# A transposition through TensorE: fewer semaphore instructions and copies on VectorE, and a semaphore by which TensorE tells that a chunk is copied

## The chip, the core and the metric

The kernel runs on one core of one Trainium2 chip. The metric is the device time of one execution in microseconds (us), lower is better. "Span" is the time from the first to the last instruction of a profiled execution; the device time lies a little above it.

## The reference

```python
def setup_inputs():
    return {"x": np.random.randn(8192, 8192).astype(np.float32)}

def reference(x):
    return np.transpose(x)
```

268 MB are read and 268 MB are written; every element moves to its mirrored place.

## The kernel before, in words

**Tiling.** The input is read in 128 chunks (`T`), t = 0 to 127. A chunk is 128 rows by 4096 columns, 2 MB. In SBUF it is 16 pieces (`NR`) of 256 columns. TensorE transposes a piece with two 128x128 matmuls against the identity (every second column each), so a chunk is 32 transposes. Pieces 0 to 7 land in one half of PSUM (`pss[0]`), pieces 8 to 15 in the other (`pss[1]`). ScalarE copies the first half out, VectorE the second (`copies`, L265).

**Why the copies go to two places.** A store should write long rows. Store w therefore collects one piece from each of 16 successive chunks. The piece of chunk t that completes store t is the direct cell: it goes straight from PSUM into the store's place in `arena`. It lies in ScalarE's half if t mod 16 is below 8, else in VectorE's. All other pieces wait in `slots`. When a store's last chunk is near, VectorE copies its 15 waiting pieces from `slots` to `arena` (`gather`, L240), some 2.4 us in two or three copies. A gather first waits until the stores that held its place have landed (`free`, on `s_st`).

**One queue.** SyncE issues all transfers in the order of the list `order`: store t-1, then load t+2, and at the end 15 shorter stores that flush what is left (`flush`). A load takes one of three places in `arena`, free once TensorE has transposed the chunk that stood there. The store of chunk t waits for its direct cell (`s_x`).

**TensorE's order in chunks 12 to 125** (`transposes`, L350; `E` = 12, `LAST` = 126): it waits until ScalarE has released its half of PSUM (`s_free[0]`), then VectorE its half (`s_free[1]`, L358); it runs two idle matmuls of 512 columns (L360), takes ScalarE's go (`s_go`, L362) and the load (`s_ld`, L363), and transposes (L366). After 4, 8, 12 and 16 pieces it raises `s_pe`: these are the four steps that the copies wait for.

**ScalarE's fillers.** From chunk 24 on (`CALM`), ScalarE waits for the load of chunk u, writes the identity twice over its own half of PSUM (L401, 2048 columns each), and only then gives `s_go`. In program order on ScalarE the fillers of chunk u stand behind its copies of chunk u-1.

**Semaphores around the copies.** Each engine counts its finished copies in `s_cp`, one per chunk, waits for its own count, and then releases its half of PSUM with an instruction of its own:

```python
                cp.then_inc(s_cp[e], 1)
                if t < T - 1:
                    eng.wait_ge(s_cp[e], t + 1)
                    eng.sem_inc(s_free[e], 1)
```

A gather waits for both counts ahead of its first copy. A chunk's copies wait for the gather's count (`s_g`) ahead of everything else.

Of the kernel before, what the change touches and what calls it, by code (L numbers as in the profile page):

```python
# [40 lines left out]
def kernel(  # L41
# [5 lines left out]
    nc = tc.nc  # L47
# [6 lines left out]
    NR = 16  # L54
# [3 lines left out]
    T = (M // J) * CH  # L58
    PIECE = B * P
    FIN = 38  # L60
    E = 12
# [13 lines left out]
    def lane(w):  # L75
        return w % W if w < T else W + w - T
# [14 lines left out]
    order = []  # L91
# [19 lines left out]
    for k in order:  # L111
        if k[0] == "L":
            wanted.append((due[k] - 2 * NR, k, NR, due[k] + 2 * NR))
        elif k[1] < T:
            w = k[1]
# [6 lines left out]
    for _, k, size, until in sorted(wanted):  # L122
        if k[0] == "L":
            o = spot(k[1])
        else:
            w = k[1]
            lo = NIN * NR if w < T - 2 else 0
            hi = END
            late = lambda o: max([f for _, a, z, f in users if a < o + size and o < z], default=0)
# [7 lines left out]
            o = min(at, key=lambda o: (late(o), o))  # L137
# [10 lines left out]
    with tc.tile_critical():  # L148
# [8 lines left out]
        s_st = [nc.alloc_semaphore(f"s_st{k}") for k in range(2 * W - 1)]  # L157
        s_pe = nc.alloc_semaphore("s_pe")
# [2 lines left out]
        s_g = nc.alloc_semaphore("s_g")  # L161
        s_go = nc.alloc_semaphore("s_go")
        s_rest = nc.alloc_semaphore("s_rest")
        s_x = [nc.alloc_semaphore("s_xa"), nc.alloc_semaphore("s_xv")]

        stored = [0] * (2 * W - 1)
# [3 lines left out]
        gathered = [0]  # L170
        closed = {}
        shut = [0, 0]

# [61 lines left out]
        def direct(w, t):  # L237
            return t == w or (t == T - 1 and w == T)

        def gather(w, upto):  # L240
            from_ = begun.get(w, max(0, w - W + 1))
            begun[w] = upto
            for u in before.pop(("S", w), []):
                free(nc.vector, u)
            r = w % NR
            runs = runs_of(
                [(slot(r, t), *place(w, t)) for t in range(from_, upto)],
                lambda a, b: (b[0] - a[0], P) if b[1] - a[1] == P and a[2] == b[2] else None,
            )
            if runs:  # L250
                for k in range(2):
                    nc.vector.wait_ge(s_cp[k], upto)  # L252
            for v in runs:
                so, do, dist = v[0]
                gap = v[1][0] - so if len(v) > 1 else PIECE
                cp = nc.vector.tensor_copy(  # L256
                    out=ap(arena, do, [[P, len(v)], [dist, B], [1, P]]),
                    in_=ap(slots, so, [[gap, len(v)], [P, B], [1, P]]),
                )
            if runs:  # L260
                cp.then_inc(s_g, 1)
                gathered[0] += 1
            ready[w] = gathered[0]

        def copies(t):  # L265
            for e, eng in enumerate((nc.scalar, nc.vector)):
                need = max(ready[w] for w in (t, T) if w in ready and direct(w, t))
                if need:
                    eng.wait_ge(s_g, need)
                first, last = e * NR // 2, (e + 1) * NR // 2  # L270
                cells_ = []
                for g in range(first, last):
                    r = range_at(t, g)
                    w = t + (r - t) % NR
                    n = next(n for n, hi in enumerate(steps(t)) if g < hi)
                    cells_.append((g, w, None if direct(w, t) else slot(r, t), n))
                runs = runs_of(
                    cells_, lambda a, b: None if None in a + b or a[3] != b[3] else b[2] - a[2]
                )
                runs.sort(key=lambda v: v[0][1] != t)  # L280
                for v in runs:
                    g, w, o, n = v[0]
                    eng.wait_ge(s_pe, 4 * t + n + 1)  # L283
                    u = g - first
                    i = pss[e][:, u * PIECE:(u + len(v)) * PIECE]
                    if o is None:
                        off, dist = place(w, t)
                        dst = ap(arena, off, [[dist, B], [1, P]])
                        i = i.rearrange("p (b i) -> p b i", b=B)
                    else:  # L290
                        gap = v[1][2] - o if len(v) > 1 else PIECE
                        dst = ap(slots, o, [[gap, len(v)], [1, PIECE]])
                        i = i.rearrange("p (l i) -> p l i", l=len(v))
                    cp = eng.copy(out=dst, in_=i) if e == 0 else eng.tensor_copy(out=dst, in_=i)  # L294
                    if w == t:
                        cp.then_inc(s_x[e], 1)
                        shut[e] += 1
                        closed[t] = (s_x[e], shut[e])
                cp.then_inc(s_cp[e], 1)
                if t < T - 1:  # L300
                    eng.wait_ge(s_cp[e], t + 1)
                    eng.sem_inc(s_free[e], 1)  # L302

        def store(w):
            if w < T:
                nc.sync.wait_ge(*closed[w])
            else:
                if w == T:
                    nc.sync.wait_ge(s_cp[0], T)
                nc.sync.wait_ge(s_g, ready[w])  # L310
            pieces = []
            base = home["S", w] * PIECE
            r = w % NR
            for a, z in parts(w):
                s, c = divmod(a, CH)
                rows = (z - a) * P
                j0 = s * J + r * PIECE
                dst = out[j0:j0 + PIECE, c * P:c * P + rows]
                dst = dst.rearrange("(q b) i -> q b i", q=P)
                pieces.append((rows, dst, arena[:, base:base + B * rows]))  # L320
                base += B * rows
            for rows, dst, src in sorted(pieces, key=lambda v: -v[0]):
                if w:
                    st = wide_dma(nc, nc.sync, "qSPDynamicHW", dst, src)
                else:
                    st = nc.sync.dma_start(out=dst, in_=src.rearrange("q (b i) -> q b i", b=B))
                st.then_inc(s_st[lane(w)], 16)
                stored[lane(w)] += 16
            done[w] = stored[lane(w)]
# [20 lines left out]
        def transposes(t):  # L350
            o = home["L", t]
            for g in range(NR):
                h, u = divmod(g, NR // 2)
                if u == 0 and not (h and E <= t < LAST):
                    nc.tensor.sem_inc(s_free[h], -1).wait_op(s_free[h], 1, "sem-ge")
                if g == 0:
                    if E <= t < LAST:
                        nc.tensor.sem_inc(s_free[1], -1).wait_op(s_free[1], 1, "sem-ge")  # L358
                        for _ in range(IDLE):
                            nc.tensor.matmul(out=pss[1][:, :4 * P], lhsT=ident, rhs=four, start=True, stop=True)  # L360
                    if E <= t < LAST:
                        nc.tensor.sem_inc(s_go, -1).wait_op(s_go, 1, "sem-ge")  # L362
                    nc.tensor.sem_inc(s_ld[o], -16).wait_op(s_ld[o], 16, "sem-ge")  # L363
                q = (o + range_at(t, g)) * PIECE
                for b in range(B):
                    tr = nc.tensor.transpose(  # L366
                        pss[h][:, (u * B + b) * P:(u * B + b + 1) * P],
                        arena[:, q + b:q + PIECE - B + b + 1:B],
                        ident,
                    )  # L370
                if g + 1 in steps(t):
                    tr.then_inc(s_pe, 1)
# [19 lines left out]
        def work(t):  # L392
            while worked[0] <= t:
                u = worked[0]
                if E <= u < LAST:
                    if u < CALM:
                        nc.scalar.sem_inc(s_go, 1)
                    else:
                        nc.scalar.wait_ge(s_ld[home["L", u]], 16)
                    for k in range(REST if u >= CALM else 0):  # L400
                        cp = nc.scalar.copy(  # L401
                            out=pss[0].rearrange("p (k i) -> p k i", i=P), in_=ap(ident, 0, [[0, J // 2 // P], [1, P]])
                        )
                        if k < REST - 1:
                            cp.then_inc(s_rest, 1)
                            rested[0] += 1
                            nc.scalar.wait_ge(s_rest, rested[0])
                    if u >= CALM:
                        cp.then_inc(s_go, 1)
                gather(u, u)  # L410
                if u == T - 1:
                    gather(T, u)
                copies(u)
                worked[0] += 1
# [10 lines left out]
                    gather(k[1], T)  # L425
                store(k[1])
        for k in range(2 * W - 1):
            nc.sync.wait_ge(s_st[k], stored[k])


# [28 lines left out]
```

## Time and profile before

| | |
|---|---|
| device time, three runs | 1265.3, 1285.86, 1289.19 us; median 1285.86 |
| profiled execution | 1273.26 us, span 1271.5 us |
| TensorE, matmuls / weight loads | 861.4 us (68%) / 655.3 us (52%) |
| VectorE | 615.1 us (48%), 715 instructions |
| ScalarE | 638.9 us (50%), 606 instructions |
| DMA | 537.07 MB, 422 GB/s over the span |
| mean granted TensorE clock | 0.869 |

How to read it: busy shares are means over the whole span. Names in rows are those of the program: L256 is the gather's copy, L294 the copies out of PSUM, L401 the fillers, L360 the idle matmuls, L366 the transposes, L28 a store's issue, L203 a load's. In a row of the timeline stand the start, the busy time, engine, line, operation and count, and in brackets the idle time ahead of it and what ended it. In a row of stretches stand, after the stretch and its length, busy times and instruction counts of PE, weight loads, VectorE, ScalarE and GpSimd, then the granted TensorE clock, the DMA share and GB/s.

### The profile page before, as it was taken

The numbers are of one execution on the slowest core, as the hardware profiler recorded it, in microseconds if no ns is written. First come the engines' busy times: TensorE is split into PE (matmuls) and PEld (weight loads), VectorE is DVE, ScalarE is ACT, GpSimd is POOL, SyncE is SP. The second block draws the span as 40 slices with busy tenths as digits, with TensorE's granted clock in tenths as the row PEclk, the third lists the DMA queues.
The fourth block names the chain that finished last, engine by engine and source line by source line (L and its number), as shares of the span: only waits on it lengthen the run. The fifth ranks groups of instructions, "written<-read, shape, count | busy, mean of one in ns | idle before, by whom it ended". The sixth has DMA issues, their size and how long they took to land. (4 is left out here: it accounts for less than half of the span.)

```text
span 1271.5 us, 12053 instructions
## 1 busy us (share of the span) xinstructions
PE 861.4 (68%) x4552; PEld 655.3 (52%) x4552; DVE 615.1 (48%) x715; ACT 638.9 (50%) x606; POOL 0.7 (0%) x6
## 2 busy tenths in 40 slices
PE   6766767777667766777767777667767667767630
PEld 5755645555545555555555555545555555455420
DVE  3554554455444454444545444554445545445481
ACT  2321224556565566555655565565655656555510
POOL 0000000000000000000000000000000000000000
PEclk9898887889898889888898888988898988889875
DMA  9999999999999999999999999999999999999998
GB/s 387 425 425 426 426 428 426 431 431 430 432 429 431 433 430 430 430 432 421 416 428 428 431 430 431 430 431 432 415 429 430 421 409 404 423 430 432 405 400 335
DMA packets 41332, 537.07 MB, mean 422 GB/s; under 512 B 4576, under 2 KB 5216, under 8 KB 8288
## 3 DMA queue, kind: packets, MB, share of 16 engines
q1 hardware_dynamic: 41312, 536.89, 99.8%
q14 instruction: 18, 0.15, 0.0%
q8 instruction: 2, 0.03, 0.0%
HBM read 268.44 MB, written 268.44 MB: 422 GB/s over the span
## 5 line engine op out<-in xcount | busy, mean ns | idle before, releaser
L366 PEld LDWEIGHTS ps<-ident,arena 128*128 128x128 f32 x4096 | 565.0, 212 | 238.2 <-issue 238.1
L366 PE MATMUL ps<-ident,arena 128*128 128x128 f32 x4096 | 579.9, 306 | 119.9 <-PEq L363 119.1
L256 DVE COPY arena<-slots 128x2048 f32<-128x2048 f32 (+7 forms) x316 | 304.3, 1012 | 483.3 <-DMA out_dram<-arena 473.7
L360 PE MATMUL ps<-ident 128*128 128x512 f32 x456 | 287.5, 764 | 242.2 <-PEq L358 242.2
L401 ACT COPY ps<-ident 128x2048 f32<-128x2048 f32 x204 | 381.4, 1869 | 52.8 <-DMA arena<-in_x_dram 49.0
L294 ACT COPY slots<-ps 128x1024 f32<-128x1024 f32 (+2 forms) x335 | 238.6, 781 | 252.2 <-DVE arena L256 220.8
L294 DVE COPY slots<-ps 128x512 f32<-128x512 f32 (+2 forms) x336 | 289.3, 913 | 64.7 <-PE ps L366 63.5
L360 PEld LDWEIGHTS ps<-ident 128*128 128x128 f32 x456 | 90.3, 219 | 329.8 <-issue 329.8
L294 ACT COPY arena<-ps 128x256 f32<-128x256 f32 x66 | 24.5, 372 | 277.8 <-DVE arena L256 223.4
L294 DVE COPY arena<-ps 128x256 f32<-128x256 f32 x63 | 26.8, 425 | 86.1 <-PE ps L366 85.2
L294 ACT ACT_TABLE_LOAD x1 | 1.3, 1283 | 1.0 <-SPq L148 1.0
L338 POOL TENSOR_SCALAR_AFFINE_SELECT ident<-ident 128x128 f32<-128x128 f32 x1 | 0.3, 292 | 0.2 <-POOL ident L336 0.2
L336 POOL MEMSET ident<- 128x128 f32 x1 | 0.2, 204 | 0.5 <-SPq L148 0.5
L443 POOL MEMSET const-bfloat16-1.0<- 128x1 bf16 x1 | 0.1, 101 | 0.0
L443 POOL MEMSET const-uint8-127<- 128x1 uint8 x1 | 0.1, 101 | 0.0
L443 POOL MEMSET const-float32-0.0<- 128x1 f32 x1 | 0.1, 98 | 0.2 <-issue 0.2
L443 POOL MEMSET const-float32-1.0<- 128x1 f32 x1 | 0.1, 98 | 0.0
## 6 DMA issues: line engine op xcount, KB each, us to landing
arena<-in_x_dram SPq DMA_DIRECT2D x128, 2048.0 KB, 20.3
out_dram<-arena SPq DMA_DIRECT2D x98, 2048.0 KB, 16.7
out_dram<-arena SPq DMA_DIRECT2D x4, 1920.0 KB, 12.4
out_dram<-arena SPq DMA_DIRECT2D x4, 1792.0 KB, 13.2
out_dram<-arena SPq DMA_DIRECT2D x4, 1664.0 KB, 13.9
out_dram<-arena SPq DMA_DIRECT2D x4, 1536.0 KB, 13.9
out_dram<-arena SPq DMA_DIRECT2D x4, 1408.0 KB, 12.6
out_dram<-arena SPq DMA_DIRECT2D x4, 1280.0 KB, 12.9
```

Source lines behind the costliest of these rows:

```text
L256: cp = nc.vector.tensor_copy(out=ap(arena, do, [[P, len(v)], [dist, B], [1, P]]), in_=ap(slots, so, [[gap, len(v)], [P, B], [1, P]]),)
L294: cp = eng.copy(out=dst, in_=i) if e == 0 else eng.tensor_copy(out=dst, in_=i)
L336: nc.gpsimd.memset(ident, 0.0).then_inc(s_id, 1)
L338: nc.gpsimd.affine_select(out=ident, in_=ident, compare_op=mybir.AluOpType.not_equal, fill=1.0, base=0, pattern=[[-1, P]], channel_multipl ...
L360: nc.tensor.matmul(out=pss[1][:, :4 * P], lhsT=ident, rhs=four, start=True, stop=True)
L366: tr = nc.tensor.transpose(pss[h][:, (u * B + b) * P:(u * B + b + 1) * P], arena[:, q + b:q + PIECE - B + b + 1:B], ident,)
L401: cp = nc.scalar.copy(out=pss[0].rearrange("p (k i) -> p k i", i=P), in_=ap(ident, 0, [[0, J // 2 // P], [1, P]]))
L443: nc = _bacc.Bacc("TRN2", target_bir_lowering=False, num_devices=1)
```

## The change

1. For chunks 11 to 124 (`told`) the count `s_cp` and the wait behind it go: an engine's last copy of a chunk raises `s_free` itself. Whoever waited for the count now waits for a new semaphore `s_seen`, which TensorE raises at the start of chunk t+1 (t+1 from 12 on), behind both of its waits for `s_free` and ahead of the idle matmuls.
2. A gather waits ahead of its last copy alone, not its first, and for one count.
3. VectorE's copies in chunks 12 to 125: the wait for the gather moves behind the direct cell; a step is waited for once; where t mod 16 is below 8, neighbouring pieces are joined into one copy across the third and fourth step, and the copy waits for the later one. The order of the copies is by step. VectorE has 350 copies out of PSUM instead of 399.
4. ScalarE waits for the telling of chunk u-1 ahead of the fillers of chunk u.
5. At the end VectorE, not SyncE, waits for the store that is issued last.

```diff
+        def told(t):
+            return E - 1 <= t < LAST - 1
+
+        def wait_copied(eng, k, t):
+            if told(t):
+                eng.wait_ge(s_seen, t - E + 2)
+            else:
+                eng.wait_ge(s_cp[k], copied_by[k, t])
...
-            if runs:
-                for k in range(2):
-                    nc.vector.wait_ge(s_cp[k], upto)
             for v in runs:
+                if v is runs[-1]:
+                    for k in range(2 if upto == T else 1):
+                        wait_copied(nc.vector, k, upto - 1)
...
-                if need:
+                after = E <= t < LAST and e == 1
+                late = after and t % NR < first
+                if need and not after:
                     eng.wait_ge(s_g, need)
...
-                    cells_, lambda a, b: None if None in a + b or a[3] != b[3] else b[2] - a[2]
+                    cells_, lambda a, b: None if None in a + b or (a[3] != b[3] and not late) else b[2] - a[2]
                 )
-                runs.sort(key=lambda v: v[0][1] != t)
+                runs.sort(key=lambda v: (v[0][1] != t, v[-1][3]))
+                seen = -1
                 for v in runs:
-                    g, w, o, n = v[0]
-                    eng.wait_ge(s_pe, 4 * t + n + 1)
+                    g, w, o, _ = v[0]
+                    n = v[-1][3]
+                    if not after or n > seen:
+                        eng.wait_ge(s_pe, 4 * t + n + 1)
+                        seen = n
+                    if after and o is not None and need:
+                        eng.wait_ge(s_g, need)
+                        need = 0
...
+                if told(t):
+                    cp.then_inc(s_free[e], 1)
+                    continue
                 cp.then_inc(s_cp[e], 1)
+                copied[e] += 1
+                copied_by[e, t] = copied[e]
                 if t < T - 1:
-                    eng.wait_ge(s_cp[e], t + 1)
+                    eng.wait_ge(s_cp[e], copied[e])
                     eng.sem_inc(s_free[e], 1)
...
                 if w == T:
-                    nc.sync.wait_ge(s_cp[0], T)
+                    wait_copied(nc.sync, 0, T - 1)
...
                     if E <= t < LAST:
                         nc.tensor.sem_inc(s_free[1], -1).wait_op(s_free[1], 1, "sem-ge")
+                        nc.tensor.sem_inc(s_seen, 1)
...
                     else:
+                        wait_copied(nc.scalar, 0, u - 1)
                         nc.scalar.wait_ge(s_ld[home["L", u]], 16)
...
-            nc.sync.wait_ge(s_st[k], stored[k])
+            (nc.vector if k == lane(order[-1][1]) else nc.sync).wait_ge(s_st[k], stored[k])
```

More of the change, by code (lines that the diff above doesn't have):

```diff
@@ L163 @@
         s_rest = nc.alloc_semaphore("s_rest")
+        s_seen = nc.alloc_semaphore("s_seen")
         s_x = [nc.alloc_semaphore("s_xa"), nc.alloc_semaphore("s_xv")]
@@ L172 @@
         shut = [0, 0]
+        copied = [0, 0]
+        copied_by = {}
+        def told(t):
[5 more added lines that the diff above has]
+                eng.wait_ge(s_cp[k], copied_by[k, t])
         REST = 2
@@ L266, in copies @@
             for e, eng in enumerate((nc.scalar, nc.vector)):
+                first, last = e * NR // 2, (e + 1) * NR // 2
                 need = max(ready[w] for w in (t, T) if w in ready and direct(w, t))
-                if need:
+                after = E <= t < LAST and e == 1
+                late = after and t % NR < first
+                if need and not after:
                     eng.wait_ge(s_g, need)
-                first, last = e * NR // 2, (e + 1) * NR // 2
                 cells_ = []
```

## The prediction

> **What bounds the kernel now.** I read the page's parts 1 to 3 and 6 first, then the waits, then the timeline of single chunks.
>
> ```profile
> span 1271.5 us, 12053 instructions
> PE 861.4 (68%) x4552; PEld 655.3 (52%) x4552; DVE 615.1 (48%) x715; ACT 638.9 (50%) x606; POOL 0.7 (0%) x6
> ...
> GB/s 387 425 425 426 426 428 426 431 431 430 432 429 431 433 430 430 430 432 421 416 428 428 431 430 431 430 431 432 415 429 430 421 409 404 423 430 432 405 400 335
> ...
> q1 hardware_dynamic: 41312, 536.89, 99.8%
> ...
> arena<-in_x_dram SPq DMA_DIRECT2D x128, 2048.0 KB, 20.3
> out_dram<-arena SPq DMA_DIRECT2D x98, 2048.0 KB, 16.7
> ```
>
> The DMA engines are full for 99.8% of the span; no engine is above 68%. 256 transfers' worth of 2 MB pass in about 1253 us, 4.9 us each, 9.79 us for a chunk's load and store. A store lands 16.7 us after its issue, 4.9 of which are its own, so a store is issued with about 11.8 us of transfers ahead of it. That is the backlog that hides late engines.
>
> ```profile
> DVE arena L256 <- DMA out_dram<-arena: 473.7, 114, 5.9
> ...
> ACT ps L401 <- DMA arena<-in_x_dram: 49.0, 97, 1.5
> ```
>
> VectorE and ScalarE both wait for DMA: the gather (L256) for a landed store, ScalarE's two filler copies (L401) for a landed load. What matters is how long one chunk's chain through the engines is against 9.79 us. The timeline of chunks 56 to 58 (remainders 8, 9, 10 of t by 16):
>
> ```profile
> 519.69 2.35 DVE L256 COPY arena<-slots 128x1792 f32<-128x1792 f32 x2 [5.04 <-DMA out_dram<-arena]
> ...
> 522.08 0.42 DVE L294 COPY arena<-ps 128x256 f32<-128x256 f32 x1
> 522.42 2.08 DVE L294 COPY slots<-ps 128x768 f32<-128x768 f32 x2
> ...
> 524.54 3.77 ACT L401 COPY ps<-ident 128x2048 f32<-128x2048 f32 x2 [0.53 <-DMA arena<-in_x_dram]
> ...
> 524.70 3.53 PE L360 MATMUL ps<-ident 128*128 128x512 f32 x4 [1.81 <-PEq L358]
> ...
> 528.60 4.07 PE L366 MATMUL ps<-ident,arena 128*128 128x128 f32 x32 [0.37 <-PEq L363]
> 529.46 2.35 DVE L256 COPY arena<-slots 128x1792 f32<-128x1792 f32 x2 [4.96 <-DMA out_dram<-arena]
> ...
> 538.38 5.60 PE L366 MATMUL ps<-ident,arena 128*128 128x128 f32 x32 [0.72 <-PEq L363]
> ...
> 543.13 0.42 DVE L294 COPY arena<-ps 128x256 f32<-128x256 f32 x1 [1.53 <-PE ps L366]
> 543.47 2.15 DVE L294 COPY slots<-ps 128x512 f32<-128x512 f32 x3
> ...
> 544.11 3.77 ACT L401 COPY ps<-ident 128x2048 f32<-128x2048 f32 x2 [0.48 <-DMA arena<-in_x_dram]
> ```
>
> From chunk 24 on, the filler copies start when the load lands (524.54, 544.11), take 3.77 us, and only then may TensorE transpose. At 544.11 VectorE is still copying the chunk before: it ends at 545.62, so the fillers overlap 1.5 us of it. The overlap is larger where t mod 16 is 12 to 15:
>
> ```profile
> 569.56 3.98 PE L366 MATMUL ps<-ident,arena 128*128 128x128 f32 x32
> ...
> 573.48 3.77 ACT L401 COPY ps<-ident 128x2048 f32<-128x2048 f32 x2 [0.48 <-DMA arena<-in_x_dram]
> 573.65 0.42 DVE L294 COPY arena<-ps 128x256 f32<-128x256 f32 x1 [2.68 <-PE ps L366]
> 574.00 2.14 DVE L294 COPY slots<-ps 128x1024 f32<-128x1024 f32 x3
> ...
> 579.73 3.99 PE L366 MATMUL ps<-ident,arena 128*128 128x128 f32 x32
> ...
> 583.83 0.42 DVE L294 COPY arena<-ps 128x256 f32<-128x256 f32 x1 [3.04 <-PE ps L366]
> ```
>
> Here the fillers start 2.66 us before VectorE ends (576.14), and a chunk already takes 10.18 us (573.65 to 583.83). The backlog covers it.
>
> **The change, part by part.**
>
> *VectorE's fewer instructions.* Gone are waits of some 0.02 to 0.05 us each, before gathers and copies and between a copy and its release, and 49 of VectorE's 399 copies out of PSUM.
>
> ```profile
> L252 DVEq EVENT_SEMAPHORE  x157: 21/50/5335, 16.1 to 1246.8; - x157
> ```
>
> 157 x 0.05 plus twice 127 x 0.02 is about 13 us in all, under the 473.7 us in which VectorE waits for stores: 0 now. It is worth its tenth of a microsecond per chunk only if that cover goes; it lies inside the 0.20 us below.
>
> *Merged copies.* Where t mod 16 is below 8, VectorE's half holds no direct cell and its copies are joined across TensorE's third and fourth step. A joined copy starts only when all 32 transposes are done.
>
> *ScalarE's new wait.* Before, the fillers of chunk u waited for ScalarE's own copies of u-1 and for load u. Now they wait for s_seen, which TensorE raises after it has taken both releases for chunk u, VectorE's among them. So the fillers can no longer overlap VectorE's copies. Behind the fillers on ScalarE stand s_go, for which TensorE waits, and ScalarE's own copies. This closes a ring: VectorE ends chunk t; TensorE tells; fillers; transposes of t+1; VectorE's copies of t+1. The terms, for a full TensorE clock:
>
> - Release to fillers: VectorE ends at 524.50 and TensorE's idle matmuls begin at 524.70. The telling drops one instruction and adds one: 0.20 us, bounds 0.1 and 0.3.
> - Fillers 3.77 us.
> - Fillers' end to transposes: 528.31 to 528.60, 0.29 us. The idle matmuls, at most 3.6 us, run beside the fillers and cost 0.
> - Transposes 4.07 us; their end to VectorE's copy, 573.54 to 573.65, 0.11 us. Sum so far 8.44 us.
> - VectorE's work after the transposes, from these shapes (views of groups by shape):
>
> ```profile
> L294 DVE COPY slots<-ps 128x1024 f32<-128x1024 f32 x145 | 175.2, 1218 | 30.7 <-PE ps L366 29.9
> ...
> L294 DVE COPY slots<-ps 128x512 f32<-128x512 f32 x96 | 62.9, 683 | 29.7 <-PE ps L366 29.5
> ...
> L294 DVE COPY slots<-ps 128x768 f32<-128x768 f32 x47 | 44.6, 950 | 4.3 <-PE ps L366 4.1
> ```
>
> 256 more columns cost 0.27 us, and two copies in a row overlap by 0.08. Remainders 0 and 1 leave a joined 1536 columns, 1.75 us; 2 leaves 1280, 1.48; 3 about 1.38; 4 to 7 leave all 2048 columns, 2.33; 8 to 11 end 1.64 us after the transposes (543.98 to 545.62), so 1.53; 12 to 15 as above, 573.65 to 576.14, 2.46 on average. No shape over 1024 stands in the trace from PSUM: two of 1024 bound it above at 2.36. Mean of the sixteen: 1.98 us.
>
> The ring is 10.42 us, already 0.63 more than DMA's 9.79. Then the clock:
>
> ```profile
> L366 PE MATMUL ps<-ident,arena 128*128 128x128 f32 x4096 | 579.9, 306 | 119.9 <-PEq L363 119.1 <-PEq L355 0.6
> ```
>
> 579.9 us over 128 chunks is 4.53 us of transposes per chunk, 0.45 more than 4.08: the share granted at half clock. Bounds: 0, if none falls on the transposes, and 0.56, if they get the mean clock (0.88 in this stage, below). I take 0.45: ring 10.87 us.
>
> ```profile
> 562.48:565.89 3.41, 1.05 (x9) 0.85 (x7) 2.26 (x3) 2.85 (x3) 0.00 (x0) 1.00 0.98 418
> 565.89:569.31 3.42, 3.05 (x4) 1.41 (x5) 0.85 (x2) 1.57 (x1) 0.00 (x0) 0.50 1.03 441
> ...
> 240.00:1200.00 960.00, 675.15 (x3493) 502.02 (x3492) 467.12 (x541) 558.29 (x497) 0.00 (x0) 0.88 1.01 427
> ```
>
> Here a stretch of 3.41 us with 1.05 us of TensorE work is followed by one at half clock. The ring keeps such gaps: 1.7 to 2.8 us from the transposes' end to the next idle matmul (0.11, VectorE's part, 0.20). The Trainium skill ("TensorE: Matmul & The Clock Gate", Part 1: The HAM clock gate) says that the clock falls to half after at least one idle window of about 3.4 us. By that rule, read as a window without work, the ring would have none: 10.42 us, 1319 in all. By the row, a third of a window's work is not enough to keep the clock.
>
> *The last store's wait.* SyncE's waits at the end come in pairs; those behind the last store's go.
>
> ```profile
> L428 SPq EVENT_SEMAPHORE  x15: 27/28/28, 1251.0 to 1270.2; - x15
> ```
>
> Seven pairs, 0.06 us apart: -0.5 us.
>
> *Sum.* Chunk 24's copies end at 210.1, those of chunk 125 (the last behind fillers) at 1210.7:
>
> ```profile
> 208.04 2.08 DVE L294 COPY slots<-ps 128x768 f32<-128x768 f32 x2
> ```
> ```profile
> 1208.26 0.42 DVE arena L294
> 1208.68 2.07 DVE slots L294 x3
> ```
>
> 101 turns of 10.87 are 1097.9. What follows took 60.8 us before, with the backlog to drain; a ring slower than DMA empties that backlog within about eleven chunks, so this is 49 (all 11.8 gone) to 60.8, and I take 55, the middle. 210.1 + 1097.9 + 55 is 1363; plus the 1.8 us between span and device time (1273.26 against 1271.5), less 0.5: **1365 us**. Against the median shown, 1285.86, that is 6.2% slower; against the profiled execution's own time 7.2%.
>
> **The rivals.**
>
> *DMA still sets the end (not slower).* The backlog must absorb every late turn: 11.8 us over 101 turns, so the ring must stay under 9.79 + 0.12 = 9.91 us. For it: VectorE waits 4.2 us per gather today, and chunk 56's copies end at 524.50, just as the load lands (524.54), so the new wait looks free there. Against it: that would need 1.5 us for VectorE's part and the clock together, where I count 2.43. Time: 1273.3 - 0.5 = 1273 us.
>
> *The same ring at full clock.* The half-clock stretches fall on the idle matmuls, as at 565.89, where the fillers hide them. 210.1 + 101 x 10.42 + 55 + 1.3 = 1319. For it: ring and stretches are both near 10.2 us, so they could lock. Against: remainders 4 to 7 and 12 to 15 take 10.8 and drift past.
>
> *Faster.* With less work VectorE could smooth the transfers: 536.89 MB at 431 GB/s, which most slices of the page's middle show, plus 2.5 us ahead, 1.7 behind and 1.8, is 1252. But transfers have full queues already; nothing in VectorE holds them.
>
> **How the numbers follow.** Ring with half clock 0.72, ring at full clock 0.17, DMA 0.09, faster 0.02. The likeliest gives 1365. Low end 1310: full clock and the shortest tail make 1313, and the telling's low bound could take up to 10 more, of which I count a third. High end: 0.56 for the clock and 0.3 for the telling, 101 x 0.21 = 21 more, and the full tail, 6 more: 1392. A measurement of this kernel can tell about 2% from no change; that is 1312 on the slow side, and the sums of both rings lie beyond it. Slower 0.88, within 2% 0.09, faster 0.03.
>
> **What would show it.** Right: L401's idle time ended by TensorE's telling and no longer by loads; the gap from VectorE's last copy to the fillers at 0.2 us in every chunk after the first dozen; transfers' share near 90% and about 394 GB/s (536.89 MB in 1363 us); VectorE's 473.7 us behind stores more than halved; PE groups 10.4 to 11 us apart. Wrong: fillers that still start with the load's landing, which would mean that the ring is under 9.9 us and DMA keeps the bound; or turns of 10.4 us, which would put the fault in the clock term alone.

## The result and the profile after

The changed kernel takes 1357.74 us (median of six runs, 1344.76 to 1363.7), the one before 1268.86 in the runs beside it (six, 1265.29 to 1289.19). The ratio is 1.0706 with a 95% interval of 1.0635 to 1.0777: 7% slower. The forecast was 1365, within 1310 to 1392. Versions that DMA bounds scatter more from run to run than the changed one (the one before reached 1300 us, three of the experiments 1303, 1308 and 1322); the ratios leave out runs more than 1.5% above the fastest of their kernel.

The page of the changed kernel (1359.55 us, span 1357.8; the lines are those of the new program: L269 gather, L316 copies out of PSUM, L385 and L386 TensorE's wait and its telling, L388 idle matmuls, L394 transposes, L430 fillers):

```profile
span 1357.8 us, 11807 instructions
...
GB/s 392 422 429 429 427 431 432 405 382 421 380 382 390 354 413 369 355 396 368 401 407 385 398 373 407 417 370 415 365 411 422 359 400 371 401 425 350 391 379 395
...
q1 hardware_dynamic: 41312, 536.89, 97.4%
...
arena<-in_x_dram SPq DMA_DIRECT2D x128, 2048.0 KB, 12.1
out_dram<-arena SPq DMA_DIRECT2D x98, 2048.0 KB, 7.8
```

A slice is 34 us. The first seven run as before, at up to 432 GB/s; chunk 24, the first behind fillers, is at 201 us, and from the eighth slice on the rate falls to 350 to 425. A store now lands 7.8 us after its issue instead of 16.7: some 3 us of transfers are ahead of it, no longer 12. The backlog is gone, although the queue is still counted busy for 97.4%. The waits show who is late instead:

```profile
DVE arena L316 <- PE ps L394: 353.0, 62, 7.7
DVE slots L316 <- PE ps L394: 335.4, 76, 12.8
...
ACT ps L430 <- PEq L386: 301.5, 102, 4.6
...
DVE arena L269 <- DMA out_dram<-arena: 35.0, 12, 4.9
```

All 102 pairs of fillers wait for L386, TensorE's telling; before, 97 waited for a load. VectorE waits for transposes (688 us in all) and almost never for a store (35 us, before 473.7). The timeline of chunks 56 to 58 shows the ring:

```profile
560.68 0.42 DVE L316 COPY arena<-ps 128x256 f32<-128x256 f32 x1 [6.61 <-PE ps L394]
561.02 2.08 DVE L316 COPY slots<-ps 128x768 f32<-128x768 f32 x2
...
563.38 3.77 ACT L430 COPY ps<-ident 128x2048 f32<-128x2048 f32 x2 [3.39 <-PEq L386]
563.40 1.96 PE L388 MATMUL ps<-ident 128*128 128x512 f32 x4 [1.67 <-PEq L385]
...
567.45 5.55 PE L394 MATMUL ps<-ident,arena 128*128 128x128 f32 x32 [2.09 <-PEq L391]
...
572.42 2.14 DVE L316 COPY slots<-ps 128x256 f32<-128x256 f32 x3
...
574.84 3.77 ACT L430 COPY ps<-ident 128x2048 f32<-128x2048 f32 x2 [2.78 <-PEq L386]
...
578.90 4.08 PE L394 MATMUL ps<-ident,arena 128*128 128x128 f32 x32 [2.09 <-PEq L391]
...
582.06 0.42 DVE L316 COPY arena<-ps 128x256 f32<-128x256 f32 x1 [5.24 <-PE ps L394]
582.40 2.14 DVE L316 COPY slots<-ps 128x512 f32<-128x512 f32 x3
```

VectorE ends at 563.10 and again at 574.56 and 584.54: turns of 11.46 us, with the transposes mostly at half clock (5.55), and 9.98, at full clock (4.08). The fillers start 0.28 us after VectorE's end each time, and TensorE's transposes 0.30 us after the fillers'.

### The profile page after: what moved, and what is told of

Its sections match the earlier page's. It is cut to its first block, busy times and chain, and to the rows that moved or that the text cites. A ratio compares the mean times of both kernels' runs of the same rounds, so it can differ in the third digit from the quotient of the medians.

```text
span 1357.8 us, 11807 instructions
## 1 busy us (share of the span) xinstructions
PE 858.3 (63%) x4552; PEld 644.6 (47%) x4552; DVE 604.2 (44%) x666; ACT 640.7 (47%) x606; POOL 0.7 (0%) x6
## 3 DMA queue, kind: packets, MB, share of 16 engines
q1 hardware_dynamic: 41312, 536.89, 97.4%
## 5 line engine op out<-in xcount | busy, mean ns | idle before, releaser
L394 PEld LDWEIGHTS ps<-ident,arena 128*128 128x128 f32 x4096 | 550.5, 211 | 309.1 <-issue 309.1
L394 PE MATMUL ps<-ident,arena 128*128 128x128 f32 x4096 | 568.7, 302 | 189.6 <-PEq L391 188.8
L430 ACT COPY ps<-ident 128x2048 f32<-128x2048 f32 x204 | 381.4, 1870 | 304.7 <-PEq L386 301.5
L388 PE MATMUL ps<-ident 128*128 128x512 f32 x456 | 291.9, 775 | 264.8 <-PEq L385 264.8
L316 DVE COPY slots<-ps 128x256 f32<-128x256 f32 (+5 forms) x287 | 288.1, 1044 | 335.7 <-PE ps L394 335.4
L269 DVE COPY arena<-slots 128x2048 f32<-128x2048 f32 (+7 forms) x316 | 303.0, 1009 | 42.6 <-DMA out_dram<-arena 35.0
L316 ACT COPY slots<-ps 128x1024 f32<-128x1024 f32 (+2 forms) x335 | 240.1, 779 | 161.5 <-PE ps L394 155.7
L388 PEld LDWEIGHTS ps<-ident 128*128 128x128 f32 x456 | 94.2, 228 | 358.7 <-issue 358.7
L316 DVE COPY arena<-ps 128x256 f32<-128x256 f32 x63 | 26.8, 425 | 353.1 <-PE ps L394 353.0
L316 ACT COPY arena<-ps 128x256 f32<-128x256 f32 x66 | 24.5, 373 | 206.1 <-PE ps L394 155.3
## 6 DMA issues: line engine op xcount, KB each, us to landing
out_dram<-arena SPq DMA_DIRECT2D x4, 1536.0 KB, 12.5
```

The source lines that it names most:

```text
L269: cp = nc.vector.tensor_copy(out=ap(arena, do, [[P, len(v)], [dist, B], [1, P]]), in_=ap(slots, so, [[gap, len(v)], [P, B], [1, P]]),)
L394: tr = nc.tensor.transpose(pss[h][:, (u * B + b) * P:(u * B + b + 1) * P], arena[:, q + b:q + PIECE - B + b + 1:B], ident,)
L430: cp = nc.scalar.copy(out=pss[0].rearrange("p (k i) -> p k i", i=P), in_=ap(ident, 0, [[0, J // 2 // P], [1, P]]))
```

## The experiments

Theory: the ring through ScalarE's new wait. Rival A: the joined copies on VectorE are the cost by themselves. Rival B: the gathers and the direct cell, with fewer waits, disturb the transfers.

**One part undone: ScalarE's wait.**

```diff
-                if told(t):
+                if told(t) and e == 1:
                     cp.then_inc(s_free[e], 1)
...
-                        wait_copied(nc.scalar, 0, u - 1)
```

> The changed kernel, but ScalarE keeps its own count and its own release, and the fillers no longer wait for TensorE's telling; all else of the change stays. Theory (the ring through ScalarE's new wait): without that wait VectorE's copies and the fillers overlap again, no ring is above DMA's 9.79 us per chunk, and the time goes back to that of before, 1262 to 1280 us. Rival A (the joined copies, or VectorE's later release, are the cost by themselves): still 1330 us or more. Rival B (gathers or the direct cell with fewer waits disturb the transfers): between the two, with a DMA share under 99% and VectorE waiting for TensorE.

Measured: 1263.51, 1266.44, 1290.89 and 1303.26 us, median 1278.66, beside a median of 1273.57 of before (thirteen runs, 1264.66 to 1293.3); no ratio was formed, but all four lie well below rival A's 1330. The profiled execution has a span of 1261.7 us and a DMA share of 100.0%. The ring is open again. From its waits and its timeline:

```profile
DVE arena L269 <- DMA out_dram<-arena: 446.9, 114, 5.1
```
```profile
569.98 2.14 DVE L316 COPY slots<-ps 128x1024 f32<-128x1024 f32 x3
...
570.83 3.77 ACT L429 COPY ps<-ident 128x2048 f32<-128x2048 f32 x2 [0.48 <-DMA arena<-in_x_dram]
```

The fillers overlap VectorE's copies by 1.29 us (570.83 to 572.12) and start with a load. Joined copies, fewer waits and the later wait of the gather are all still in: rivals A and B fall.

**The part alone: the kernel before with ScalarE's wait.**

```diff
                         nc.tensor.sem_inc(s_free[1], -1).wait_op(s_free[1], 1, "sem-ge")
+                        nc.tensor.sem_inc(s_seen, 1)
...
+                        nc.scalar.wait_ge(s_seen, u - E + 1)
                         nc.scalar.wait_ge(s_ld[home["L", u]], 16)
```

> The kernel before, with one thing added: TensorE raises the telling, and ScalarE's fillers wait for it. Theory: this alone closes the ring. With unjoined copies VectorE's part after the transposes is 1.47 us where t mod 16 is below 8 instead of 1.97 on average, so the mean ring is 0.25 us shorter than the 10.79 measured, plus some 0.05 for the release by an instruction of its own: 10.6 us, 1335 us with bounds 1318 and 1350. Rival A (joined copies alone): no change from before, 1262 to 1280. Rival B: no change from before.

Measured: 1346.4 us (1345.83 to 1346.62), ratio 1.0579, interval 1.0518 to 1.064. One instruction on TensorE and one wait on ScalarE are most of the loss. The waits name it:

```profile
ACT ps L404 <- PEq L360: 284.0, 102, 4.8
```

The time is within the bounds, 11 us above the middle. A gap in the traces and a slip in the expectation's sum account for most of these 11 us. The first lines are of this run, the second of the changed kernel, both of a chunk whose t mod 16 is above 11:

```profile
599.28 5.55 PE L368 MATMUL ps<-ident,arena 128*128 128x128 f32 x32 [2.12 <-PEq L365]
604.94 0.42 DVE L295 COPY arena<-ps 128x256 f32<-128x256 f32 x1 [7.49 <-PE ps L368]
605.28 2.14 DVE L295 COPY slots<-ps 128x1024 f32<-128x1024 f32 x3
...
607.76 3.77 ACT L404 COPY ps<-ident 128x2048 f32<-128x2048 f32 x2 [4.55 <-PEq L360]
```
```profile
631.56 5.55 PE L394 MATMUL ps<-ident,arena 128*128 128x128 f32 x32 [2.09 <-PEq L391]
637.15 0.42 DVE L316 COPY arena<-ps 128x256 f32<-128x256 f32 x1 [7.67 <-PE ps L394]
637.49 2.08 DVE L316 COPY slots<-ps 128x1024 f32<-128x1024 f32 x2
639.85 3.77 ACT L430 COPY ps<-ident 128x2048 f32<-128x2048 f32 x2 [4.20 <-PEq L386]
```

From the transposes' end to VectorE's copy it is 0.11 us with the semaphore instructions of before and 0.04 in the changed kernel; from VectorE's end to the fillers it is 0.34 and 0.28. The expectation allowed 0.05 for the second gap and nothing for the first: that is 0.07 us a turn, some 7 of the 11. The sum itself was short as well: 101 turns of 0.2 us less than 1357.74 give about 1338, not 1335.

**One part undone: joining.**

```diff
-                late = after and t % NR < first
+                late = False
```

> The changed kernel, with VectorE's copies not joined across the third and fourth step; all else stays. Theory: VectorE's part after the transposes falls to a mean of 1.74 us from 2.00, so 101 turns of 10.53 us instead of 10.79: 26 us less than the changed kernel, 1332 us, bounds 1315 and 1345. Rival A (joined copies alone): back to 1262 to 1280. A rival by which joining costs nothing in the ring: 1357.

Measured: 1334.48 us (1331.4 to 1340.94), ratio 1.0494, interval 1.0424 to 1.0564: 23 us less than the changed kernel, where 26 were worked out. This version and the one with the telling alone both have the ring and unjoined copies; they differ by the rest of the change, VectorE's fewer instructions above all, and by 12 us. So these instructions are worth some 0.12 us a turn inside the ring: adding ScalarE's wait costs 73 us (1273.57 to 1346.4), the rest of the change gains 12, joining costs 23.

**Joining alone, in the kernel before.**

```diff
+                late = e == 1 and E <= t < LAST and t % NR < first
...
-                    cells_, lambda a, b: None if None in a + b or a[3] != b[3] else b[2] - a[2]
+                    cells_, lambda a, b: None if None in a + b or (a[3] != b[3] and not late) else b[2] - a[2]
...
-                    g, w, o, n = v[0]
+                    g, w, o, _ = v[0]
+                    n = v[-1][3]
```

> The kernel before, with the joined copies alone. Theory: VectorE ends later by up to 0.9 us in half of the chunks, which the backlog of transfers covers, since the fillers don't wait for it: no change, 1262 to 1280 us. Rival A (joined copies alone are the cost): 1290 us or more.

Measured: 1272.91 us (median of eleven runs, 1265.29 to 1308.1), ratio 0.9995, interval 0.9952 to 1.0038. Rival A is excluded a second time: without the ring the backlog covers the later copies, and joining costs only inside it.

**A shorter ring, with the wait in place.**

```diff
-        REST = 2
+        REST = 1
```

> The changed kernel with one filler copy per chunk instead of two; the new wait stays. Theory: the ring is 1.9 us shorter, 10.79 - 1.90 = 8.9 us, below DMA's 9.79, so DMA sets the end again and the wait costs nothing: 1262 to 1285 us. A rival by which the wait itself (TensorE's extra instruction, a late telling) costs 0.8 us per chunk whatever the ring's length: 1340 us or more.

Measured: 1267.67, 1271.08, 1297.37 and 1322.06 us, median 1284.23, beside a median of 1268.55 of before (seven runs, 1265.48 to 1300.02); span of the profiled execution 1265.9 us. No ratio was formed, and the median lies only just within the expected range, but all four runs lie below the rival's 1340.

```profile
DVE arena L269 <- DMA out_dram<-arena: 508.1, 114, 5.9
...
ACT ps L430 <- PEq L386: 118.1, 100, 2.7
```

The fillers still wait for the telling in 100 of 102 chunks, but VectorE waits for stores again. So the wait itself is not the price: it costs only when the ring that it closes is longer than DMA's 9.79 us.

**The clock term.** Three idle matmul calls per chunk, and none:

```diff
-        IDLE = 2
+        IDLE = 3
```

> The changed kernel with three idle matmul calls per chunk instead of two; 2.94 us at full clock, still beside the fillers. Tests the clock term: more work by TensorE in each 3.41 us should leave fewer stretches at half clock, so that the transposes come nearer to 4.08 us from 4.46; against it, idle matmuls at half clock would outlast the fillers by up to 0.6 us. Theory: 1325 to 1355, 1345 as the middle, with a granted clock above 0.91. If the clock share doesn't depend on TensorE's work: 1358 to 1375.

Measured: 1339.97 us (1335.55 to 1346.81), ratio 1.0576, interval 1.0517 to 1.0636, mean granted clock 0.898 over the span.

> The changed kernel without idle matmuls. Theory: the stretch ahead of each chunk's transposes is then without work, these begin at half clock in every chunk and take 6 to 8 us; the ring becomes 12 to 14 us: 1480 to 1680 us. If the clock share doesn't depend on TensorE's work: 1350 to 1365.

Measured: 1517.06 us (two runs), ratio 1.1963, interval 1.1906 to 1.202, clock 0.714. The groups of transposes of the two:

```profile
L394 PE MATMUL ps<-ident,arena 128*128 128x128 f32 x4096 | 526.9, 288 | 89.9 <-PEq L391 89.1
```
```profile
L394 PE MATMUL ps<-ident,arena 128*128 128x128 f32 x4096 | 750.2, 366 | 720.0 <-PEq L391 719.2
```

Per chunk these are 4.12 and 5.86 us, against 4.44 in the changed kernel. How much of the transposes runs at half clock depends on TensorE's own work. Over the chunks behind fillers alone a chunk's transposes take 6.0 us without idle matmuls, the low end of the 6 to 8 that were expected. The granted clock with three calls, 0.898 over the span and 0.91 from 240 to 1280 us, is not above the 0.91 that was expected, and little above the 0.90 of the changed kernel (240 to 1300 us). What changed is where the half clock falls: with three calls the transposes are near full speed, while the idle matmuls, beside the fillers, take 767 ns each on average, where four at full clock take 1.96 us, 490 each.

```profile
L388 PE MATMUL ps<-ident 128*128 128x512 f32 x684 | 422.4, 767 | 263.3 <-PEq L385 263.3
```

The third call also outlasts the fillers at times, as the expectation allowed for: from their end to the transposes it is 0.45 us on average instead of 0.30. The 18 us between two and three calls are a difference of medians; the runs of the two just overlap (1335.55 to 1346.81 and 1344.76 to 1363.7).

No run gave a version that clearly beats the one before.

## Why the prediction was right, step by step

**The bound.** Right: the ring sets the pace from chunk 24 on, DMA before. First and last of the 101 turns:

```profile
210.37 2.08 DVE L316 COPY slots<-ps 128x768 f32<-128x768 f32 x2
```
```profile
1300.10 2.14 DVE L316 COPY slots<-ps 128x1024 f32<-128x1024 f32 x3
```

From 212.45 to 1302.24 are 1089.8 us, 10.79 per turn; predicted 10.87. The start was 2.3 us later than in the trace of before. The tail, 1357.8 - 1302.24 = 55.6 us, was put at 55, the middle of 49 to 60.8; that it fits so closely is luck.

**The terms.** The forecast is 7 us too high. Against the profiled execution, 1359.55 us, it is 5: 8 too much in the turns, 2.3 too little at the start.

| us per turn | predicted | measured |
|---|---|---|
| release to fillers | 0.20 | 0.28 (563.10 to 563.38) |
| fillers | 3.77 | 3.77 |
| fillers to transposes | 0.29 | 0.30 (567.15 to 567.45) |
| transposes with half clock | 4.52 | 4.44 (568.7 / 128, below) |
| transposes' end to VectorE's copy | 0.11 | 0.04 (637.11 to 637.15) |
| VectorE's part | 1.98 | 1.96 (the rest of 10.79) |

```profile
L394 PE MATMUL ps<-ident,arena 128*128 128x128 f32 x4096 | 568.7, 302 | 189.6 <-PEq L391 188.8 <-PEq L382 0.8
```

The release was sized too low, 0.08 a turn or 8 us in all: that one instruction goes and one comes was taken as even. With the telling alone (second experiment) the gap grew from 0.20 to 0.34; what VectorE no longer does took back only 0.06. The 0.11 from the transposes' end to VectorE's copy was read from the kernel before, and it too shrank with VectorE's instructions, by 0.07. The prediction counted 13 us of such instructions, put them at 0 in the kernel before and inside the 0.20 in the ring; the ring shows them, about 0.13 us a turn, in two places.

The clock's share, 0.45 predicted and 0.37 measured, was carried over from a kernel that DMA paces, without a reason why a ring should have the same. One call of idle matmuls more makes it almost nothing and none makes it 1.8 us (4.12 and 5.86, less 4.08), so its fit is in part luck. It also moves from run to run: the six runs of the changed kernel stand in the order of their mean granted clock, from 1344.76 us at 0.915 to 1363.7 at 0.874.

**Joined copies.** The lengths worked out from shorter ones hold: 1.75 us for 1536 columns, and for 2048 in one copy a little less than the bound of 2.36.

```profile
L316 DVE COPY slots<-ps 128x1536 f32<-128x1536 f32 x21 | 36.9, 1758 | 42.1 <-PE ps L394 42.1
...
L316 DVE COPY slots<-ps 128x2048 f32<-128x2048 f32 x7 | 16.0, 2292 | 43.1 <-PE ps L394 43.1
```

**The clock rule.** By the rule that the prediction weighed (the Trainium skill, "TensorE: Matmul & The Clock Gate", Part 1: The HAM clock gate: half clock after an idle window of about 3.4 us), read as a window without work, the time would have been 1319. Stretches of the changed kernel (columns as in the prediction):

```profile
550.62:554.03 3.41, 1.89 (x4) 0.68 (x4) 3.41 (x3) 1.88 (x2) 0.00 (x0) 1.00 1.07 375
554.03:557.45 3.42, 1.33 (x11) 1.30 (x11) 0.04 (x1) 1.86 (x1) 0.00 (x0) 1.00 0.85 331
557.45:560.86 3.41, 3.41 (x18) 3.41 (x17) 0.18 (x1) 2.03 (x2) 0.00 (x0) 0.50 0.70 298
```

The first stretch, with 1.89 us of work, kept the clock; the second, with 1.33 us, lost it. Without idle matmuls there are stretches without any work, and there the rule holds too:

```profile
567.41:570.82 3.41, 0.00 (x0) 0.00 (x0) 3.41 (x5) 1.68 (x1) 0.00 (x0) 1.00 1.16 428
570.82:574.23 3.41, 1.03 (x5) 1.06 (x6) 0.38 (x1) 2.06 (x2) 0.00 (x0) 0.50 0.93 341
```

So an empty stretch is enough but not needed, and the row was the better guide. The whole trace of the changed kernel, where changes of the clock lie whole multiples of 3.41 us apart, can be cut into such stretches: from full clock, 70 stretches with at most 1.64 us of work were followed by half clock and 232 with at least 1.50 by full clock; from half clock, 69 with at least 2.75 us were followed by full clock and 23 with at most 2.77 by half. In this trace a stretch that is a little under half busy keeps the clock, but it takes one some four fifths busy to win it back.

**The last store's wait.** SyncE's last wait is over at 1354.5, ahead of the end, and then it waits 2.0 us for VectorE:

```profile
L457 SPq EVENT_SEMAPHORE  x15: 17/28/28, 1337.9 to 1354.5; - x15
```
```profile
SPq L148 <- DVEq L148: 2.0, 1, 2.0
```

The waits behind the last store are gone, as predicted: from the last transfer's end to the end of the span it is 1.5 us, before 2.1. That is too little for any ratio here to show.

**Wrong:** the sign that transfers' share would be near 90%. The rate is as forecast (396 GB/s against 394), the share 97.4%. The gap to the fillers is 0.28 us, not 0.2. And the single turns do not lie between 10.4 and 11 us, as the sign for TensorE's groups had it; they run from 9.85 to 12.5, and only their mean of 10.79 does.

## What to carry to other kernels

When a semaphore is replaced by another that comes later or by way of another engine, list everything that had to be done before the old one and before the new one: an event that also waits for a third engine can close a ring through engines that overlapped before. Add up the ring and compare it with the present bound per turn; slack absorbs a few late turns, but not a hundred. What costs nothing under one bound, like VectorE's 13 us of semaphore instructions here, gets its price back when the bound moves to the chain in which it stands. Where an engine merely waits for its own copies, its own count releases it without closing such a ring.

## What was not expected

The busy share of the DMA queue is a poor witness of whether DMA bounds: 97.4% at 395 GB/s in the changed kernel against 99.8% at 422. The time from a store's issue to its landing (7.8 against 16.7 us) and the waits tell it.

Two idle matmul calls per chunk, which compute nothing of the result, are worth 159 us in this ring (1517.06 against 1357.74): they keep the clock for the transposes behind them. A third takes off another 18 by the medians.
